# A batched transposing matmul: stores issued two batches sooner, and the first load of a in one transfer

## The chip, the core and the metric

One core of one Trainium2 chip. The metric is the device time in microseconds of one execution of the kernel, as the median of three runs. Five engines work side by side, each with its own instruction stream: PE (matmul), DVE (vector), ACT (scalar), POOL and SP. SP and ACT also issue DMAs, each into its own hardware queue, and 16 DMA engines serve both queues.

## The reference

Sixteen independent products of 512 x 512 matrices in float32; both operands come transposed.

```python
batch, m, k, n = 16, 512, 512, 512
a: [batch, k, m] float32        b: [batch, n, k] float32
out = np.matmul(a.transpose(0, 2, 1), b.transpose(0, 2, 1))   # [batch, m, n] float32
```

a and b are 16.8 MB each, and so is the output.

## The kernel before

Batches are handled in eight pairs (H = 8, B = 16). Every batch goes through these stages:

- **Loads (SP, q1).** b is loaded a pair at a time (2 MB, rows of 16 KB to a partition) into one of three buffers. a is loaded a pair at a time for pairs 1 to 5 (`WIDE`, 2 MB, rows of 16 KB), and a batch at a time for batches 0, 1 and 12 to 15 (1 MB, rows of 8 KB), into one of three pair buffers. Batch 0's a goes in two transfers, partitions 0 to 15 and partitions 16 to 127, both counted on the same semaphore.
- **Casts to bf16.** ACT casts a (`cast_a`, L168 and L170), DVE casts b (`cast_b`, L193).
- **Transposing b (PE, L246).** b in bf16 is seen as float32 words, so that one transpose turns two numbers at once; DVE copies the result from PSUM to SBUF (`turn`, L202).
- **Matmuls (PE, L260).** A batch is done in two halves of eight matmuls each. Each matmul group of four raises `summed` by one, so that `summed` is 4 for every finished batch.
- **Copies out (L180).** DVE copies the first half from PSUM into the output buffer, ACT the second half. There are five output buffers of one pair each (`OUTS`).
- **Stores (L89).** A pair is stored in one transfer of 2 MB (rows of 8 KB). Pairs 0 to 4 are stored from ACT's queue (q10): in `run_act`, behind the copy out of batch i, the pair j is stored for which i = 2j + 1 + LAG. With LAG = 3 pair 0 is stored behind the copy of batch 4. Pairs 5, 6 and 7 are stored by SP, behind all its loads; pair 7 in two transfers of one batch each.

Everything is ordered by hand with semaphores, and each engine runs its own program in order. What the steps of the prediction touch:

- ACT's order for batch i is: cast of batch i + 1, copy out of batch i (which waits until PE has summed all four parts of batch i), then possibly a store.
- DVE's order for pair p is: cast of the first half of pair p + 1's b, copy out of batch 2p, turn; cast of the other half, copy out of batch 2p + 1, turn.
- SP's order is that of the batches. Ahead of the loads of a for batches 10, 12 and 14 it waits until the store of pair 0, 1 and 2 has landed (its output buffer is to be used again). Ahead of a load into a used buffer of a it waits for PE (`summed`), and ahead of a b for the transposes (`turned`).
- SP's stores at the end wait for `summed`: pair 5 for the third part of batch 12, pair 6 for the third part of batch 14, the first half of pair 7 for the first part of batch 15, its second half for the last copies.

Of the kernel before, what the change touches and what calls it, by code (L numbers as in the profile page):

```python
# [11 lines left out]
def kernel(  # L12
# [7 lines left out]
    P = 128  # L20
    B, K, M = a.shape
    _, N, _ = b.shape
    KO = K // P
# [12 lines left out]
    a_v = a.rearrange("b (ki ko) m -> b ki ko m", ko=KO)  # L36
# [4 lines left out]
    WIDE = range(1, 6)  # L41
    LOADS = 3
    PAIRS = 3
    OUTS = 5
    LAG = 3
    TAIL = 3
    H = B // 2
    STORED = H - (H - OUTS) + 1
# [5 lines left out]
    with tc.tile_critical(sync_engine=nc.gpsimd.engine):  # L54
# [3 lines left out]
        a_sb = [sb(f"a_sb{s}", [P, 2 * KO, M], f32) for s in range(LOADS)]  # L58
# [12 lines left out]
        a_in = [sem(f"a_in{s}") for s in range(2 * LOADS)]  # L71
# [22 lines left out]
        def load_a(sp, i):  # L94

            q, g = divmod(i, 2)
            s, use = q % LOADS, q // LOADS
            if use:

                sp.wait_ge(summed, MO * (2 * (q - LOADS) + 1) + 1)  # L100
            if i == 0:

                for part in (slice(0, 16), slice(16, P)):
                    sp.dma_start(a_sb[s][part, :KO], a_v[0, part]).then_inc(a_in[0], 16)
            elif q in WIDE:
                sp.dma_start(a_sb[s][:], a_w[q]).then_inc(a_in[2 * s], 16)
            else:
                sp.dma_start(a_sb[s][:, g * KO:(g + 1) * KO], a_v[i]).then_inc(a_in[2 * s + g], 16)

        def loaded_a(q, g):  # L110

            g = 0 if q in WIDE else g
            uses = [u for u in range(q + 1) if u % LOADS == q % LOADS and (g == 0 or u not in WIDE)]
            return a_in[2 * (q % LOADS) + g], 16 * (len(uses) + (q % LOADS + g == 0))

        def run_sp(sp):
            for i in range(B):
                if i == 0:
                    load_a(sp, 0)


                for p in ([0] if i == 0 else [(i + 1) // 2] if i % 2 and i + 1 < B else []):
                    if p >= PAIRS:
                        sp.wait_ge(turned, p - PAIRS + 1)
                    sp.dma_start(b_sb[p % PAIRS][:], b_v[p]).then_inc(b_in[p % PAIRS], 16)
                if i % 2 == 0 and i // 2 >= OUTS:

                    sp.wait_ge(o_out[i // 2 % OUTS], 16 * (i // 2 // OUTS))
                if i and not (i % 2 and i // 2 in WIDE):
                    load_a(sp, i)  # L130

            for j in range(H - TAIL, H - 1):
                sp.wait_ge(summed, MO * (2 * j + 2) + 3)
                store(sp, j)

            sp.wait_ge(summed, MO * (B - 1) + 1)
            sp.wait_ge(half_go, 1)
            store(sp, H - 1, slice(0, 1))
            sp.wait_ge(last_go, 3)
            store(sp, H - 1, slice(1, 2))  # L140
# [17 lines left out]
        def cast_a(act, i):  # L158


            q, g = divmod(i, 2)
            sem_, value = loaded_a(q, g)
            x, to = a_sb[q % LOADS], a_bf[i % 2]
            act.wait_ge(sem_, value)
            if q in WIDE:
                own = slice(g * P // 2, (g + 1) * P // 2)
                for s in range(2):
                    copy = act.copy(to[s * P // 2:(s + 1) * P // 2], x[own, s * KO:(s + 1) * KO, :])  # L168
            else:
                copy = act.copy(to[:], x[:, g * KO:(g + 1) * KO, :])  # L170
            copy.then_inc(ac_go, 1)

        def copy_out(eng, i, rm, go):

            q = rm if isinstance(rm, int) else rm.stop - 1
            eng.wait_ge(summed, MO * i + q + 1)
            copy = eng.copy if eng is nc.scalar else eng.tensor_copy
            h = q // 2
            p = rm - 2 * h if isinstance(rm, int) else slice(None)
            copy(o_sb[i // 2 % OUTS][:, i % 2, rm, :], o_ps[h][:, p, :]).then_inc(go, 1)  # L180
# [40 lines left out]
        def run_act(act):  # L221
            cast_a(act, 0)
            for i in range(B - 1):
                cast_a(act, i + 1)
                copy_out(act, i, slice(2, 4), oa_go)
                j, odd = divmod(i - LAG, 2)
                if odd and 0 <= j < H - TAIL:
# [94 lines left out]
```

## Time and profile before

| | |
|---|---|
| median of 3 runs | 125.56 us (125.41 to 125.62) |
| the profiled execution | 125.41 us, span 123.5 us |
| mean granted TensorE clock | 0.948 |
| PE busy | 83.8 us (68%) |
| ACT busy | 66.9 us (54%) |
| DVE busy | 56.0 us (45%) |
| bytes moved | 50.33 MB |
| first store's issue on ACT | 45.0 us |
| last copy out ends | 114.5 us |

The span runs from the first to the last profiled instruction; what lies around it is 1.9 us. In the page's strip of 40 slices a slice is 3.1 us, and a digit is a share in tenths. A row of the group table has busy time, mean duration and the idle time ahead of it with the one that ended it. A row of a queue has packets, MB and the time of its packets as a share of 16 engines' time. In a table by stretch the columns are PE, PE's weight loads, DVE, ACT and POOL busy time with the number of instructions, then the granted clock, the DMA engines' share and GB/s.

### The profile page before, as it was taken

What the parts mean: (1) busy time and instruction counts of PE and PEld (TensorE: products, weight loads), DVE (VectorE), ACT (ScalarE), POOL (GpSimd) and SP (SyncE); (2) the same over time, 40 slices, a digit from 0 to 9 for tenths busy, and PEclk for the clock granted to TensorE, in tenths of its full rate; (3) what the DMA queues carried; (4) which work ended last, traced back from release to release, by engine and by line L of the source; (5) the groups of instructions that cost most, each with busy time, mean ns of one, the idle gap of its engine ahead of it and who ended that gap; (6) DMA issues with size and microseconds to landing.
All of it is one profiled execution on the core that took longest, in us unless ns stands there. A gap on an engine that the chain in (4) does not pass through costs nothing. (4 is left out here: it accounts for less than half of the span.)

```text
span 123.5 us, 1086 instructions
## 1 busy us (share of the span) xinstructions
PE 83.8 (68%) x392; PEld 48.1 (39%) x400; DVE 56.0 (45%) x48; ACT 66.9 (54%) x44; POOL 0.7 (1%) x6
## 2 busy tenths in 40 slices
PE   0000749799979979997996950595999499798000
PEld 0000733275546437445644620133744364374000
DVE  0002552829575592965759340039296543703000
ACT  4060006293999799799889008995320773803000
POOL 2000000000000000000000000000000000000000
PEclk9999999999999999999999999559999999999955
DMA  5989999999999999999999999999999999999992
GB/s 88 337 382 440 430 424 430 435 430 424 424 424 424 424 424 432 411 430 432 454 390 456 422 440 419 427 422 462 393 424 435 424 427 432 427 427 427 427 424 90
DMA packets 4944, 50.33 MB, mean 407 GB/s; under 512 B 464, under 2 KB 464, under 8 KB 464
## 3 DMA queue, kind: packets, MB, share of 16 engines
q1 hardware_dynamic: 3584, 39.85, 77.3%
q10 hardware_dynamic: 1360, 10.49, 20.1%
HBM read 33.55 MB, written 16.78 MB: 407 GB/s over the span
## 5 line engine op out<-in xcount | busy, mean ns | idle before, releaser
L260 PE MATMUL o_ps<-bt_sb,a_bf 128*128 128x512 bf16 x248 | 64.1, 407 | 9.5 <-PEq L235 8.5
L260 PEld LDWEIGHTS o_ps<-bt_sb,a_bf 128*128 128x128 bf16 x256 | 29.0, 116 | 39.9 <-issue 18.3
L168 ACT CAST a_bf<-a_sb 64x2048 bf16<-64x2048 f32 x20 | 38.0, 1898 | 6.8 <-DMA a_sb<-in_a_dram 6.5
L246 PE MATMUL bt_ps<-identity,b_bf 128*128 128x128 f32 x144 | 22.1, 302 | 20.5 <-PEq L235 20.5
L180 DVE COPY o_sb<-o_ps 128x1024 f32<-128x1024 f32 x16 | 19.6, 1224 | 30.7 <-PE o_ps L260 30.7
L246 PEld LDWEIGHTS bt_ps<-identity,b_bf 128*128 128x128 f32 x144 | 20.5, 209 | 25.4 <-issue 24.2
L193 DVE CAST b_bf<-b_sb 128x2048 bf16<-128x2048 f32 x16 | 19.4, 1219 | 22.9 <-DMA b_sb<-in_b_dram 22.9
L180 ACT COPY o_sb<-o_ps 128x1024 f32<-128x1024 f32 (+1 forms) x17 | 16.4, 965 | 19.7 <-PE o_ps L260 19.6
L170 ACT CAST a_bf<-a_sb 128x2048 bf16<-128x2048 f32 x6 | 11.4, 1900 | 20.2 <-DMA a_sb<-in_a_dram 20.2
L202 DVE COPY bt_sb<-bt_ps 128x1024 f32<-128x1024 f32 x16 | 19.4, 1215 | 2.7 <-PE bt_ps L246 2.7
L170 ACT ACT_TABLE_LOAD x1 | 1.3, 1283 | 0.9 <-PEq L306 0.9
L147 POOL TENSOR_SCALAR_AFFINE_SELECT identity<-identity 128x128 f32<-128x128 f32 x1 | 0.3, 296 | 0.2 <-POOL identity L145 0.2
L145 POOL MEMSET identity<- 128x128 f32 x1 | 0.2, 205 | 0.7 <-POOLq L54 0.7
L306 POOL MEMSET const-uint8-127<- 128x1 uint8 x1 | 0.1, 103 | 0.0
L306 POOL MEMSET const-bfloat16-1.0<- 128x1 bf16 x1 | 0.1, 102 | 0.0
L306 POOL MEMSET const-float32-0.0<- 128x1 f32 x1 | 0.1, 99 | 0.2 <-issue 0.2
L306 POOL MEMSET const-float32-1.0<- 128x1 f32 x1 | 0.1, 99 | 0.0
## 6 DMA issues: line engine op xcount, KB each, us to landing
b_sb<-in_b_dram SPq DMA_DIRECT2D x8, 2048.0 KB, 20.2
a_sb<-in_a_dram SPq DMA_DIRECT2D x5, 2048.0 KB, 18.3
out_dram<-o_sb ACTq DMA_DIRECT2D x5, 2048.0 KB, 16.2
a_sb<-in_a_dram SPq DMA_DIRECT2D x5, 1024.0 KB, 16.7
out_dram<-o_sb SPq DMA_DIRECT2D x2, 2048.0 KB, 13.3
out_dram<-o_sb SPq DMA_DIRECT2D x2, 1024.0 KB, 8.9
a_sb<-in_a_dram SPq DMA_DIRECT2D x1, 896.0 KB, 5.6
a_sb<-in_a_dram SPq DMA_DIRECT2D x1, 128.0 KB, 3.1
```

The lines of the kernel that those rows point to most:

```text
L145: pool.memset(identity[:], 0.0).then_inc(id_go, 1)
L147: pool.affine_select(out=identity[:], in_=identity[:], compare_op=mybir.AluOpType.not_equal, fill=1.0, base=0, pattern=[[-1, P]], channel_ ...
L168: copy = act.copy(to[s * P // 2:(s + 1) * P // 2], x[own, s * KO:(s + 1) * KO, :])
L170: copy = act.copy(to[:], x[:, g * KO:(g + 1) * KO, :])
L180: copy(o_sb[i // 2 % OUTS][:, i % 2, rm, :], o_ps[h][:, p, :]).then_inc(go, 1)
L193: dve.tensor_copy(to, x).then_inc(bc_go, n)
L202: dve.tensor_copy(bt_sb[g][:].rearrange("p j (ni r) -> p j ni r", r=NR), bt_ps[:].rearrange("p j r (g ni) -> p g j ni r", g=2)[:, g],).the ...
L246: last = pe.transpose(bt_ps[:, j, r, :], w[:, r, j, :], identity[:])
L260: last = pe.matmul(o_ps[h][:, q, :], a_r[:, rk, 2 * h + q, :], bt_h[:, rk // 2, rk % 2, :], start=(rk == 0), stop=(rk == KO - 1),)
L306: nc = _bacc.Bacc("TRN2", target_bir_lowering=False, num_devices=1)
```

## The change

Two edits. LAG goes from 3 to 1, so that the store of pair j is issued by ACT behind the copy out of batch 2j + 2 instead of batch 2j + 4. And batch 0's a is loaded by one transfer of 128 partitions, as the other single batches are, with its semaphore count adapted.

```diff
-    LAG = 3
+    LAG = 1
...
-            if i == 0:
-
-                for part in (slice(0, 16), slice(16, P)):
-                    sp.dma_start(a_sb[s][part, :KO], a_v[0, part]).then_inc(a_in[0], 16)
-            elif q in WIDE:
+            if q in WIDE:
                 sp.dma_start(a_sb[s][:], a_w[q]).then_inc(a_in[2 * s], 16)
             else:
                 sp.dma_start(a_sb[s][:, g * KO:(g + 1) * KO], a_v[i]).then_inc(a_in[2 * s + g], 16)
...
-            return a_in[2 * (q % LOADS) + g], 16 * (len(uses) + (q % LOADS + g == 0))
+            return a_in[2 * (q % LOADS) + g], 16 * len(uses)
```

The loop that LAG steers, the same before and after:

```python
            for i in range(B - 1):
                cast_a(act, i + 1)
                copy_out(act, i, slice(2, 4), oa_go)
                j, odd = divmod(i - LAG, 2)
                if odd and 0 <= j < H - TAIL:
                    store(act, j)
```

## The prediction

> **What bounds the kernel now.** I read the page first: the forty slices and the DMA queues.
>
> ```profile
> span 123.5 us, 1086 instructions
> ...
> DMA  5989999999999999999999999999999999999992
> ...
> q1 hardware_dynamic: 3584, 39.85, 77.3%
> q10 hardware_dynamic: 1360, 10.49, 20.1%
> HBM read 33.55 MB, written 16.78 MB: 407 GB/s over the span
> ```
>
> The DMA engines are busy in all slices but the first and the last. q1 is SP's queue (33.55 MB of loads and the last three pairs' stores), q10 is ACT's (five stores of 2.10 MB). From 12 us to 121 us the table by stretch gives 422 to 431 GB/s whatever the mixture, so I use 424. The bytes don't change; the end can only move if engines idle at the start, or run dry at the end. So next the tail, in the out_dram answer and the timeline.
>
> ```profile
> L89 SPq DMA_DIRECT2D out_dram<-o_sb x4: 344/366/403, 94.7 to 114.5; - x4
> DMA to landing us min/median/max: 8.0/14.4/18.3
> ```
>
> ```profile
> 96.37 1.90 ACT L170 CAST a_bf<-a_sb 128x2048 bf16<-128x2048 f32 x1 [3.60 <-DMA a_sb<-in_a_dram]
> ...
> 98.57 2.00 PE L260 MATMUL o_ps<-bt_sb,a_bf 128*128 128x512 bf16 x8 [0.90 <-PEq L235]
> ...
> 113.90 0.59 ACT L180 COPY o_sb<-o_ps 128x512 f32<-128x512 f32 x1 [0.32 <-PE o_ps L260]
> ```
>
> The last store (batch 15, 1.05 MB) is issued at 114.5 and lands 8.0 us later, at 122.5. The engines stop moving bytes at 121.1 (the stretch 121 to 122 has a share of 0.07), and 1.05 MB takes 2.5 us, so its bytes began at about 118.7: it stood 4.2 us behind other stores. That is the tail's whole cover. The first two lines of the timeline are the start of the last uninterrupted run of compute: batch 13's a lands at 96.4, ACT casts it at once, PE starts its first half 2.2 us after the landing, and from there to the last issue is 114.5 - 98.57 = 15.9 us with no wait for a load. So the last issue is batch 13's landing plus 18.1 us.
>
> How the queues share is read in the stretches around the first store, issued on ACT at 45.0: 44.8 to 48.5, 48.5 to 55.5, and 63.2 to 66.7 after a load was issued at 63.31.
>
> ```profile
> q1 hardware_dynamic: 115, 1.62, 103.1%
> ```
>
> ```profile
> q1 hardware_dynamic: 132, 1.90, 63.5%
> q10 hardware_dynamic: 128, 1.05, 35.3%
> ```
>
> ```profile
> q10 hardware_dynamic: 180, 1.47, 99.5%
> ```
>
> For 3.5 us after its issue the store moves nothing. Then loads of 16 KB rows get 1.90 MB in 7 us and the store 1.05 MB: about 2 to 1. The two loads that landed beside stores did so 7.4 us apart (55.7, 63.2) against 4.9 us alone (33.8, 38.7, 43.5). Beside loads of 8 KB rows (batches 12 to 15) it is near 1 to 1. In the third stretch q1 is empty: today SP waits for store 0 to land before it issues pair 5's a.
>
> ```profile
> SPq L108 <- DMA out_dram<-o_sb: 17.7, 2, 12.0
> SPq L106 <- DMA out_dram<-o_sb: 15.3, 1, 15.3
> ```
>
> **The change, part by part.** *The stores.* Store j of the five is issued when PE ends batch 2j+2 instead of 2j+4. No instruction and no semaphore wait is added; an issue takes 0.38 us on ACT's queue and moves ahead of two casts and two copies, while the ACT engine still works off its cast, so I cost that at nothing (uncovered it would be 0.4 us). What moves is bandwidth. PE ends batch 2 at 34.4 (32.68 + 1.75 in the timeline): store 0 is issued there, and moves bytes from 34.4 + 3.5 = 38, against 48.6 now. From then on loads go at the shared pace. Pair 3's b still lands at 38.7; behind it, 7.4 us each: pair 3's a 46.3 (now 43.5), b of pair 4 53.7 (48.4), its a 61.1 (55.7), b of pair 5 68.5 (63.2), its a 75.9, b of pair 6 83.3. Pair 5's a comes 1.4 us later only (now 74.5), since store 0 lands at 38 + 14.7 = 52.7 (14.7 us, as from 48.6 to 63.3 now) and SP issues that load then, not at 63.3: q1 doesn't run empty.
>
> Does q10 stay full? Stores start at 38, 52.7, 67.4, 82.1. Store 1 is issued at 45.0, store 2 at 55.5 (PE's end of batches 4 and 6; pair 3's a at 46.3 is before its cast at 47.04). Batch 8 needs the a that lands at 61.1: casts of 3.8 us, then two halves of 1.9, so store 3 is issued at 68.7. Batch 10 needs the a of 75.9: 75.9 + 3.8 + 3.8 gives store 4 at 83.5. All are there in time, so stores run without a break to the end of the loads. SP's gates for the remaining loads (store 1 landed, 67.4, for batch 12; store 2 landed, 82.1, for batches 14 and 15) also come before their turn in the queue.
>
> Then batch 12 at 1 to 1, 4.9 us: 88.2 (now 85.25). b of pair 7, 7.4: 95.6 (91.1). Batch 13, 4.9: 100.5 (96.35). Today store 3 begins to move only at 88.2 and store 4 at 99.9, so batch 13 passes with three and a half stores done; now it passes with almost all five. Batch 13 is 4.15 us later, bounds 3 (stores a little slower) and 6 (all five through). Pair 7's b doesn't bind: cast 1.2, copy 1.2, turn 1.2, transposes 1.2 end near 100.6, the cast of batch 13 at 102.4. Batch 14's a (105.0, cast 106.9) is before its need at 107.6, batch 15's (107.5) too. So the last issue goes to 114.5 + 4.15 = 118.7.
>
> Meanwhile the stores that covered it are gone: behind the last load only stores 5, 6 and 7 are left, 6.3 MB or 14.8 us. The last store's bytes begin at 118.7 + L, where L is the latency from issue to bytes, against 118.7 now. The loss is 4.15 + L - 4.2, about L. The trace has L at 3.5 us with the engines full (the store above), where most of it may be queueing, and about 1.0 with them idle:
>
> ```profile
> GB/s 0 0 0 0 0 0 0 0 0 0 0 0 0 0 0 590 459 0 0 328 393 131 0 131 131 66 66 0 328 524 197 524 459 393 328 328 131 459 393 66
> ```
>
> This is the first 5 us in slices of 0.125: the first load, issued at 0.89, moves at 1.9. Engines about to run dry are nearer to the idle row; as store 7's first half is still in flight I take 1.6. The tail costs 4.15 + 1.6 - 4.2 = 1.55 us, with ends at 0 (batch 13 only 3 us later, L 1.0: covered) and 5.3 (6 and 3.5). Store 6 goes at 106.3 + 4.15 = 110.5 plus L, as store 5's bytes end at about 111.2: a gap of 0.9, swallowed by the later one.
>
> The Trainium skill's page "DMA: Bandwidth & Descriptors", section "Latency and other measured facts", puts the first byte of such a transfer at about 600 ns; the trace's idle row is longer, 1.0, and its full row longer still. By that figure the tail would cost about 0.55 us, an estimate from that page.
>
> *The first load.* Two transfers (16 partitions, then 112) become one; SP saves one issue of 0.45 us, and everything behind goes out that much sooner. In the slices above, 131 KB move at 1.9 to 2.1, nothing for a quarter of a microsecond, and the bulk starts at 2.45. In one transfer the bulk can start at about 2.0, with 131 KB more in it (0.31 us at 424 GB/s): net -0.14. Bounds: -0.45 (the early piece bought nothing) and +0.31 (the larger transfer starts no sooner). I take -0.1. It is seen in full, for the whole span follows it.
>
> Sum against the profiled execution: 125.41 + 1.55 - 0.1 = 126.9 (the span 123.5 becomes 125.0, 1.9 lies around it). The median of the runs is 0.15 above that execution; I leave it inside the rounding.
>
> **Rivals.** *The PE clock falls in the last run of compute.* Once in this trace PE had nothing for 5.9 us:
>
> ```profile
> 72.70:76.60 3.90, 0.07 (x1) 0.00 (x0) 0.00 (x0) 2.06 (x2) 0.00 (x0) 1.00 1.01 431
> 76.60:83.40 6.80, 4.77 (x12) 1.70 (x13) 1.25 (x2) 6.55 (x4) 0.00 (x0) 0.50 1.00 426
> ```
>
> The granted clock fell 3.9 us into it and came back 4.8 us after matmuls resumed at 78.63. In the new timing batch 12's matmuls end between 97.1 and 99.2 and batch 13's start at 102.7, so 3.4 to 5.6 us without a matmul, against 3.0 now (95.6 to 98.57). If it falls, 4.8 us at half clock lose 2.4: 129.3. Against it: an earlier stall at pair 6 moves batch 12 towards 99.2. The Trainium skill, "TensorE: Matmul & The Clock Gate", section "Part 4: PE-mode transpose", says that transposes don't count as busy for this clock; the start of this trace agrees (16 transposes from 13.1, yet matmuls at half pace until 22.0). By that rule pair 7's transposes between the two don't keep the clock; if they did, this rival would fall away.
>
> *The tail stays covered.* If store 4 or 3 is late, or batch 13 is under 3 us later, no engine runs dry: 125.41 with the start's -0.1, so 125.3 to 125.6. For it: the full DMA digits of the profile. Against it: cover of 4.2 less L is all there is.
>
> *Faster.* One mechanism: the removed issue brings the bulk of the loads forward by the whole 0.45 us, at the start, and the tail is covered: 125.41 - 0.45 = 125.0. It decides if the late chain slips by less than 4.2 - L.
>
> **Chances.** Forecast 0.53, clock 0.2, covered 0.17, faster 0.1. A measurement can tell about 0.2% from no change, 0.25 us. The range goes from 125.3 (covered) to 129.3 (clock; L at 3.5 alone gives 128.8). Faster 0.1; same 0.13, most of the covered case; slower 0.77, with the rest of it.
>
> **What would show it.** Right: q10 moves from about 38 us; pair 3 to 5 loads 7.4 us apart and pair 5's a issued near 53; batch 13 landed near 100.5, the last issue near 118.7, and a dip in the DMA digits behind 111 us. Wrong: the last issue at 116 or sooner, or no dip (covered); a clock of 0.5 between 100 and 108 us (clock); the first bytes' bulk later than 2.45 us (the split was worth something).

## The result and the profile after

The changed kernel takes 128.34 us (128.15 to 128.5, 4 runs) against 125.52 us (4 runs): a ratio of 1.0225, 95% interval 1.0207 to 1.0242. The direction and the main mechanism of the forecast hold; the loss is 2.8 us where 1.3 were forecast. The profiled execution took 128.15 us, 2.7 more than the one of before.

The page of the changed kernel: span, clock and DMA in 40 slices of 3.16 us, and the stores' rows.

```profile
span 126.3 us, 1085 instructions
...
PEclk9999999999999999769999959999999855999996
DMA  3999999999999999999999999999999999909975
...
out_dram<-o_sb ACTq DMA_DIRECT2D x5, 2048.0 KB, 20.4
...
out_dram<-o_sb SPq DMA_DIRECT2D x2, 2048.0 KB, 10.6
out_dram<-o_sb SPq DMA_DIRECT2D x2, 1024.0 KB, 4.4
```

There is a hole now in the DMA row, the 0 at slice 36, from 110.5 to 113.7 us, and the last two slices (7 and 5) aren't full either. SP's small stores land 4.4 us after their issue (the median) instead of 8.9: they hardly stand behind others any more.

The table by stretch of the changed kernel shows the hole; the last three columns are clock, DMA share and GB/s.

```profile
106.00:110.00 4.00, 3.93 (x20) 2.23 (x19) 2.36 (x2) 0.60 (x1) 0.00 (x0) 0.89 1.01 428
110.00:114.00 4.00, 3.92 (x17) 1.74 (x16) 1.73 (x2) 2.81 (x2) 0.00 (x0) 1.00 0.18 74
114.00:118.00 4.00, 3.13 (x19) 2.27 (x19) 0.64 (x2) 1.01 (x1) 0.00 (x0) 1.00 1.03 426
118.00:122.00 4.00, 2.65 (x15) 1.52 (x14) 1.21 (x1) 1.17 (x2) 0.00 (x0) 1.00 0.87 360
```

From 110 to 114 us PE works all the time, while the DMA engines have 0.18 of their time filled: nothing is left to move until PE has summed enough of batch 14 for store 6. Before the change the share was full to 121 us:

```profile
100.00:108.00 8.00, 7.07 (x34) 3.73 (x33) 4.71 (x4) 5.57 (x4) 0.00 (x0) 1.00 1.02 431
108.00:121.00 13.00, 5.72 (x31) 3.79 (x32) 1.22 (x1) 1.43 (x3) 0.00 (x0) 0.87 1.01 428
```

The timeline of the changed kernel at batch 13, and the out_dram answer for SP's stores:

```profile
101.99 1.90 ACT L166 CAST a_bf<-a_sb 128x2048 bf16<-128x2048 f32 x1 [6.94 <-DMA a_sb<-in_a_dram]
...
104.19 3.23 PE L256 MATMUL o_ps<-bt_sb,a_bf 128*128 128x512 bf16 x8 [1.50 <-PEq L231]
```

```profile
L89 SPq DMA_DIRECT2D out_dram<-o_sb x4: 345/367/403, 97.0 to 121.4; - x4
```

Batch 13's a lands at 102.0 (96.4 before); the cast had waited 6.9 us for it. The first half of batch 13 starts 2.2 us after the landing, as before, but takes 3.23 us instead of 2.00. The last store is issued at 121.4, not 114.5: 6.9 us later, of which 5.6 are the landing and 1.2 the slower half.

### The profile page after: what moved, and what is told of

Read it like the earlier page. It is cut to its first block, busy times and chain, and to the rows that moved or that the text cites. A ratio compares the mean times of both kernels' runs of the same rounds, so it can differ in the third digit from the quotient of the medians.

```text
span 126.3 us, 1085 instructions
## 1 busy us (share of the span) xinstructions
PE 84.5 (67%) x392; PEld 49.1 (39%) x400; DVE 56.1 (44%) x48; ACT 66.7 (53%) x44; POOL 0.7 (1%) x6
## 3 DMA queue, kind: packets, MB, share of 16 engines
q10 hardware_dynamic: 1360, 10.49, 19.6%
## 5 line engine op out<-in xcount | busy, mean ns | idle before, releaser
L242 PE MATMUL bt_ps<-identity,b_bf 128*128 128x128 f32 x144 | 23.3, 313 | 26.9 <-PEq L231 26.9
L189 DVE CAST b_bf<-b_sb 128x2048 bf16<-128x2048 f32 x16 | 19.5, 1221 | 32.5 <-DMA b_sb<-in_b_dram 32.5
L242 PEld LDWEIGHTS bt_ps<-identity,b_bf 128*128 128x128 f32 x144 | 21.4, 210 | 31.9 <-issue 30.8
L198 DVE COPY bt_sb<-bt_ps 128x1024 f32<-128x1024 f32 x16 | 19.4, 1215 | 2.3 <-PE bt_ps L242 2.3
```

Of the source, the lines that this page charges most:

```text
L189: dve.tensor_copy(to, x).then_inc(bc_go, n)
L198: dve.tensor_copy(bt_sb[g][:].rearrange("p j (ni r) -> p j ni r", r=NR), bt_ps[:].rearrange("p j r (g ni) -> p g j ni r", g=2)[:, g],).the ...
L242: last = pe.transpose(bt_ps[:, j, r, :], w[:, r, j, :], identity[:])
```

## The experiments

Times are medians; each ratio is to the kernel before on the same chip (125.4 to 125.5).

**Each part alone.** First only the first load:

```diff
-    LAG = 1
+    LAG = 3
```

> Only the first load in one transfer, LAG stays 3. Theory (the start's gain is real, 1.1 us by the landings of b for pair 0, 10.60 against 11.70, and the engines' work at the end still covers the last store): 125.5 - 1.1 = 124.4, 124.2 to 124.8. Rival (as predicted, the start is worth 0.1 us and the earlier landings are given back): 125.2 to 125.6.

Measured: 124.39 us, ratio 0.9914 (0.989 to 0.9938). The theory holds: the first load in one transfer is worth 1.1 us where the end is covered. Batch 13's a lands at 96.6, and the last store, issued at 116.8, still stands behind others.

Then only the stores, on the kernel before:

```diff
-    LAG = 3
+    LAG = 1
```

> Only LAG 1, the first load stays in two transfers. Theory (the end hangs on batch 13's a, which lands when its own bytes and those of all the stores ahead of it are through; a start 1.1 us later delays the stores too, so fewer of their bytes come ahead of it): 128.0 to 129.0, the start's gain hardly seen. Rival (the two parts simply add): 128.3 + 1.1 = 129.4, 129.2 to 129.8.

Measured: 128.57 us, ratio 1.0249 (1.0182 to 1.0317), with executions from 127.8 to 129.6. The median fits the theory and is below what adding would give, but 129.4 would be a ratio of 1.031, inside the interval: that the parts don't simply add is not shown. Batch 13's a landed at 102.5, 0.5 us later than in the changed kernel, and that landing differs by more from one execution to the next (101.2 to 102.7, below). The theory's reason doesn't hold: up to that landing q10, the stores' queue, had moved 10.48 MB, against 10.49 MB in the changed kernel, so the later start left no fewer bytes of stores ahead of it.

**What sets the end.** TAIL 4 takes store 4 from ACT's queue and puts it behind SP's loads; the other four stores stay early.

```diff
-    TAIL = 3
+    TAIL = 4
```

> The changed kernel with TAIL 4: store 4 goes behind the loads on SP's queue, stores 0 to 3 stay early on ACT's. Theory (what counts is the bytes of stores ahead of batch 13's a and the bytes left behind the last load): batch 13's a lands about 5 us sooner, near 97, the engines don't run dry, 124.4, 124.2 to 124.8. Rival (early stores slow the loads and stall the compute all the way, whatever is left for the end): 126.5 to 128.3.

Measured: 124.54 us, ratio 0.9927 (0.9903 to 0.995). The whole loss is gone, though store 0 goes at 33.6 us (sooner than with LAG 1 and the split load, 34.8) and the loads beside the stores are as slow as in the changed kernel. Batch 13's a landed at 96.7. The same stretches as above, of this kernel:

```profile
106.00:110.00 4.00, 3.66 (x16) 1.58 (x14) 2.12 (x2) 2.92 (x3) 0.00 (x0) 1.00 1.01 428
110.00:114.00 4.00, 3.47 (x22) 2.67 (x23) 0.65 (x2) 0.71 (x1) 0.00 (x0) 1.00 1.02 430
114.00:118.00 4.00, 2.25 (x12) 1.13 (x11) 0.82 (x1) 1.17 (x2) 0.00 (x0) 1.00 1.01 426
118.00:122.00 4.00, 0.00 (x0) 0.00 (x0) 0.00 (x0) 0.00 (x0) 0.00 (x0) 0.76 0.63 264
```

The share stays at 1.01 to 1.02 until 118. Early stores as such do no harm here; what does is that all five are through ahead of batch 13's a.

Then half the step:

```diff
-    LAG = 1
+    LAG = 2
```

> The changed kernel with LAG 2. Theory: stores start 5 us later than with LAG 1, 0.75 MB fewer ahead of batch 13's a, which lands some 1.8 us sooner (near 100.2); the gap of the engines ahead of store 6 shrinks by as much: 126.4, 125.6 to 127.2. Rival (a threshold: any earlier store does the whole damage, or none): 128.3 or 124.4.

Measured: 124.38 us, ratio 0.9911 (0.9888 to 0.9934). My number was missed, and the time is the one that I gave to "none of the damage". The trace says why: batch 13's a landed at 98.3, not 100.2 (store 0 goes at 38.1 us, 6.7 later than with LAG 1; store 4 lands at 104.9, well behind batch 13's a, and 1.29 MB fewer of stores come ahead of it, not 0.75), and the last store goes at 117.8. The DMA rows of this kernel from 110 to 124 us, in slices of 0.35 us:

```profile
DMA  9999889999898999998999927998999900000000
GB/s 468 515 398 398 374 374 421 492 515 398 374 421 374 374 468 562 398 398 374 398 398 421 445 94 304 421 398 374 374 374 374 375 0 0 0 0 0 0 0 0
```

The 2 at the 24th slice, 118.1 us, is the moment at which store 7's first half ends and the second has just been issued. LAG 2 uses up the cover to the last tenths and pays nothing. So it is no threshold in the stores but the end of a cover, which is larger than I had it. The profiles give its size (the third column is what q10 had moved when batch 13's a landed):

| kernel | store 0 issued | q10 by then, MB | batch 13's a landed | last store issued | span | span behind the last issue |
|---|---|---|---|---|---|---|
| before | 45.0 | 8.06 | 96.4 | 114.5 | 123.5 | 9.0 |
| first load whole, LAG 3 | 42.1 | 8.39 | 96.6 | 116.8 | 122.4 | 5.6 |
| LAG 1, TAIL 4 | 33.6 | 8.39 | 96.7 | 117.0 | 122.7 | 5.7 |
| LAG 2 | 38.1 | 9.20 | 98.3 | 117.8 | 122.7 | 4.9 |
| changed (LAG 1) | 31.4 | 10.49 | 102.0 | 121.4 | 126.3 | 4.9 |
| LAG 1, split load | 34.8 | 10.48 | 102.5 | 121.9 | 126.8 | 4.9 |

The landing follows the bytes of stores ahead of it, not the time of the first store. In these profiles the span is never shorter than the last issue plus 4.9 us (3.9 to the landing, 1.0 behind it), nor shorter than what I take for the engines' time for all bytes: 122.4 to 122.7 with the quick start, 123.5 with the slow one. The kernel before had 9.0 - 4.9 = 4.1 us of cover. In rows two to four the last store goes 19.5 to 20.2 us behind batch 13's landing, not 18.1, and the span doesn't show it: that is the cover at work.

**The clock.** The changed kernel's slow half at 104 us falls into a clock of 0.5. To take that away I let PE sum the last quarter of batch 12 six times (the same values) while it waits, with the last two passes of its loop written out; a control has the loop written out only. `pair` is the loop's body as a function, and hands its argument to the second half of batch 12.

```diff
-                for q in range(2):
+                for q in [0] + [1] * (1 + again):
...
-                    last.then_inc(summed, 1)
+                    if q == 0 or again == 0:
+                        last.then_inc(summed, 1)
+                    again -= q
...
-            with pe.Fori(0, H) as _i:
+            with pe.Fori(0, H - 2) as _i:
+                pair()
+            pair(5)
+            pair()
```

The control, with pair(0) in place of pair(5):

> The changed kernel with the last two passes of PE's loop written out, nothing else; the control of the next run. All theories: 128.3, 127.9 to 128.7.

Measured: 128.16 us, ratio 1.0186 (1.0149 to 1.0224), one execution at 127.29.

> As the control, and PE sums the last quarter of batch 12 six times over (five repeats of four matmuls, 4.3 us, the same values), so that it isn't without matmuls while it waits for pair 7's b and batch 13's a. Theory (the clock that fell at 100.1 us costs 1.2 us of the 2.8: the first half of batch 13 took 3.23 us against 1.99, and all of it is on the path to the last store): the clock stays at 1.0 past 104 us, the last store is issued near 120.1, 127.1, 126.8 to 127.5. Rival (the copies of DVE and ACT set the pace of the last run, not PE): 128.3.

Measured: 127.67 us, ratio 1.0184 (1.016 to 1.0208). In the trace it does what it was made for. The stretches from 100 to 106 us, of the control and then of the kernel with the repeats:

```profile
100.00:104.00 4.00, 1.58 (x10) 1.10 (x10) 0.64 (x1) 2.78 (x2) 0.00 (x0) 0.74 1.01 426
104.00:106.00 2.00, 2.00 (x7) 0.66 (x5) 0.00 (x0) 1.77 (x2) 0.00 (x0) 0.50 1.03 434
```

```profile
100.00:104.00 4.00, 4.00 (x22) 2.44 (x21) 1.25 (x2) 1.31 (x1) 0.00 (x0) 1.00 1.00 420
104.00:106.00 2.00, 1.45 (x8) 0.74 (x8) 0.00 (x0) 2.00 (x3) 0.00 (x0) 1.00 1.01 426
```

The clock stays at 1.00, and from the landing of batch 13's a (102.7) to the last issue (120.8) it is 18.1 us, as before the change; in the control it is 20.3 (101.2 to 121.5). But batch 13's a landed 1.5 us later in this execution. So both were measured again, in more executions:

> The control again, with more rounds, beside the kernel with the repeated sums: 128.2, 127.9 to 128.5 by all theories.

> The kernel with the repeated sums again, with more rounds. Theory (the clock costs 1.2 us on the path to the last store): 1.2 us below the control. Second theory (it costs that in the run of compute, but the landing of batch 13's a wanders by as much from one execution to the next, 101.2 to 102.7 us in the profiles so far, so that some 0.5 us are seen): 0.3 to 0.8 us below the control. Rival (no effect): within 0.2 us of it.

Measured: control 127.39 us, ratio 1.0155 (1.012 to 1.019), executions from 126.8 to 128.4; with the repeats 127.55 us, ratio 1.0168 (1.0134 to 1.0201), executions from 126.4 to 128.3. The control was to be near 128.2 and wasn't. Here too the trace has 18.1 us with the repeats (101.5 to 119.6) against 19.5 in the control (101.8 to 121.3). The times show no gain that can be told from none, as the rival has it; the traces show the run of compute shorter by 1.3 to 2.2 us. All ten executions of each, from both rounds, have means of 127.7 and 127.5: a gain of 0.2 us, give or take 0.6, so the 1.2 us that I gave the clock are not in the times. One thing bears on it: the two control executions that were profiled have the lowest mean granted clock of the control's ten (0.917 and 0.928; the others have 0.936 to 0.954), so the traces may show the control at its worst. The landing wanders (101.2 to 102.7 in five profiles of LAG 1 with the whole load), and not with the stores: q10 had moved 10.40 to 10.49 MB by then in all five. That this eats the gain is not shown. What the clock costs the changed kernel in the times stays open.

**Why the first load is worth 1.1 us.** Two other cuts of it, on the kernel before. By partitions in the middle:

```diff
-                for part in (slice(0, 16), slice(16, P)):
+                for part in (slice(0, 64), slice(64, P)):
```

> The kernel before with the first load cut at partition 64 instead of 16. Theory P (the 112-partition transfer is slow by its shape: its 8 KB packets took 423 ns against 309 ns of the 128-partition one, and 64 partitions spread evenly): 124.5, 124.2 to 124.8, b of pair 0 landed by 10.9. Theory I (a second issue ahead of everything, 0.45 us, and the ramp between the two transfers cost the 1.1): 125.5.

Measured: 126.49 us, ratio 1.009 (1.0065 to 1.0114). Neither theory's number: slower than the kernel before. By columns, with all partitions in each transfer:

```diff
-                for part in (slice(0, 16), slice(16, P)):
-                    sp.dma_start(a_sb[s][part, :KO], a_v[0, part]).then_inc(a_in[0], 16)
+                for part in (slice(0, KO // 2), slice(KO // 2, KO)):
+                    sp.dma_start(a_sb[s][:, part], a_v[0, :, part]).then_inc(a_in[0], 16)
```

> The kernel before with the first load in two transfers of all 128 partitions, half of the columns each (rows of 4 KB). Theory P: 124.5, 124.2 to 124.8, since both transfers have 128 partitions. Theory I: 125.5.

Measured: 124.69 us, ratio 0.9936 (0.9919 to 0.9952). So a second issue, with rows of 4 KB, costs 0.3 us; the rest is the shape. The stretch from 3.5 to 5 us, where hardly anything but this load is under way, of the kernel before (112 partitions), of the cut at 64, and of the whole load with LAG 3:

```profile
3.50:5.00 1.50, 0.00 (x0) 0.00 (x0) 0.00 (x0) 0.00 (x0) 0.00 (x0) 1.00 0.99 344
```

```profile
3.50:5.00 1.50, 0.00 (x0) 0.00 (x0) 0.00 (x0) 0.00 (x0) 0.00 (x0) 1.00 0.81 175
```

```profile
3.50:5.00 1.50, 0.00 (x0) 0.00 (x0) 0.00 (x0) 0.00 (x0) 0.00 (x0) 1.00 1.02 431
```

They move 344, 175 and 431 GB/s. In the second the engines are only 0.81 busy, as the first half ends there and the other begins; for a full share it would be 347, 216 and 423 GB/s. So a transfer over fewer partitions is slower for every byte, and 64 are worse than 112. It is the size of the loss, too: from 2 to 8 us the whole load's kernel moved 2.34 MB, the cut by columns 2.20, the kernel before 1.89 and the cut at 64 1.57. At 424 GB/s the last three are 0.3, 1.1 and 1.8 us behind the first, and their times are 0.3, 1.1 and 2.1 us longer. Why fewer partitions are slower no run shows. The Trainium skill's page "DMA: Bandwidth & Descriptors", section "Rules for kernel authors", says of two transfers to disjoint partition halves not to bother, since they serialize. These runs agree with the advice, and the price is more than waiting in line: the two halves cost 126.49 - 124.39 = 2.1 us.

Last, whether the start can be quicker still, with b of pair 0 issued by ACT (LAG 3, first load whole):

```diff
-                for p in ([0] if i == 0 else [(i + 1) // 2] if i % 2 and i + 1 < B else []):
+                for p in ([] if i == 0 else [(i + 1) // 2] if i % 2 and i + 1 < B else []):
...
         def run_act(act):
+            act.dma_start(b_sb[0][:], b_v[0]).then_inc(b_in[0], 16)
             cast_a(act, 0)
```

> LAG 3, first load whole, and b of pair 0 issued on ACT's queue beside it. If the ramp of the first microsecond is the issue order of SP, b of pair 0 and everything behind it come some 0.3 us sooner: 124.1, 123.9 to 124.3. Rival (the ramp is the engines' own first packets, 0.5 to 1.3 us each): 124.4 as with the whole first load alone.

Measured: 124.42 us, ratio 0.9912 (0.9895 to 0.9929): the rival's number, nothing gained. Pair 0's b came later, at 12.1 us for 10.7, as it now shares the engines with batch 0's a. The last store was issued at 114.0, 2.8 us sooner than with the whole load alone, and the span is no shorter for it (122.7 for 122.4): the end is covered. The best that was found is the first load whole at LAG 3 or 2 (124.4 us, 1.1 us under the kernel before), with LAG 1 and TAIL 4 next to it (124.5).

## Why the prediction came out as it did

**Right:** that the bytes set a floor and only the two ends can move the time; that stores two batches sooner slow the loads (7.3 to 7.6 us apart from pair 3's b to pair 6's); that pair 5's a is issued early, at 50.9, with q1 never empty; that the cover behind the last load is then gone. Q10 was full to the end, as worked out. A gap ahead of store 6 was forecast at 0.9 us; the engines stood still for some 3 us. TAIL 4 shows the mechanism by undoing it.

**The step that failed:** "Batch 13 is 4.15 us later", and "the last issue goes to 114.5 + 4.15 = 118.7". It went to 121.4, 6.85 later. Two terms make the 2.7 us that were missed:

*The landing* is 5.6 us later, close to the bound of 6 ("all five through"). These rows are what q10 had moved from the span's start to batch 13's landing, before and in the changed kernel:

```profile
q10 hardware_dynamic: 1032, 8.06, 19.8%
```

```profile
q10 hardware_dynamic: 1360, 10.49, 24.3%
```

Before, 3.8 stores were through and not "three and a half"; now all five are, 2.43 MB more, which is 5.7 us at 424 GB/s. My 4.15 us are 1.76 MB. I had given every store 14.7 us, so that store 4 would start at 96.8. The run with LAG 1 and the split load checks that, since its store 0 goes at 34.8, about where I had it (34.4): its stores landed at 53.4, 67.4, 81.4, 93.0 and 103.7. The first three are as forecast; store 3 took 11.6 us, beside loads with rows of 8 KB, for which my own rows had near 1 to 1. Its row and that of store 2 (issued at 70.19 and 55.85; the last number is us to landing):

```profile
out_dram<-o_sb ACTq DMA_DIRECT2D x1, 2048.0 KB, 25.5
```

```profile
out_dram<-o_sb ACTq DMA_DIRECT2D x1, 2048.0 KB, 22.8
```

So store 4 started some 4 us sooner than in my sum and was as good as through. (A slip of 0.2: pair 3's a is 38.7 + 7.4 = 46.1, not 46.3.)

*The run of compute* is 1.2 us longer in this trace, 19.4 us for 18.1. That is the rival to which I gave 0.2, at half its price of 2.4, and its sign is there: 6.3 us without a matmul (97.9 to 104.2), transposes between them, and the clock at 0.51 from 100 to 104 us. I had set it aside because an earlier stall would push batch 12 to 99.2; it ended at 97.9. Whether the times, and not only the traces, carry its 1.2 us is the point left open above.

In the changed kernel store 0 went at 31.4, 3.0 us sooner than I had it: 1.1 are the quicker start of the stream, which I held for 0.1, and 1.6 the first batch's matmuls, as the transposes and matmuls of the start show, before and then changed:

```profile
13.10 3.66 PE L246 MATMUL bt_ps<-identity,b_bf 128*128 128x128 f32 x16 [13.10 <-PEq L235]
18.51 5.42 PE L260 MATMUL o_ps<-bt_sb,a_bf 128*128 128x512 bf16 x16 [1.75 <-PEq L235]
```

```profile
11.99 3.29 PE L242 MATMUL bt_ps<-identity,b_bf 128*128 128x128 f32 x16 [11.99 <-PEq L231]
17.04 3.81 PE L256 MATMUL o_ps<-bt_sb,a_bf 128*128 128x512 bf16 x16 [1.76 <-PEq L231]
```

PE's pace doubled at 22.0 us before and at 14.7 in the changed kernel; this is read from its instructions, since the profile's clock column has 1.00 in both stretches. That head start is not what makes batch 13 late: with the split load there is none, and the bytes of stores ahead are the same. But the start speaks against the rule on transposes that I took up in the clock rival and found confirmed in the kernel before. In the changed kernel the pace rose when PE had run nothing but transposes, and all sixteen matmuls behind them ran at the full pace.

**The cover** was mis-sized the other way: 4.2 - 1.6 = 2.6 us in my sum, 4.1 by the profiles, partly because the latency from issue to bytes with idle engines is shorter than I took. The last store is 8.0 us from issue to landing before, and 3.9 where nothing stands ahead of it. Store 6 shows the latency: it is issued at 113.2 us, and this is the DMA row of the changed kernel from 108 to 116 us in slices of 0.2.

```profile
DMA  9898898899894630000000000000009399399696
```

The engines stand still until 114.0 to 114.2: some 0.9 us behind the issue, so the idle row (1.0) was the right one and my 1.6 too much by 0.7. The other 0.8 I put down to the 118.7 at which I had the last store's bytes begin: it rests on 121.1 as their end, and a few still moved until about 121.7 (a share of 0.04 from 121.5 to 122). The sum with the measured terms: 5.6 + 1.2 - 4.1 = 2.7, the difference of the two profiled executions. The cover's error took 1.5 us off the two others: the forecast would have been farther off without it, and that is luck.

**The start** was mis-sized by ten times, -0.1 for -1.1, and outside my bounds of -0.45 and +0.31: I priced the bytes and the issue and took the rate of 112 partitions for that of 128, though the kernel's own second stretch stood at 252 GB/s between 2.5 and 5 us. And "seen in full, for the whole span follows it" holds where the end is covered. In the changed kernel 0.2 us of it are left by the medians (128.34 for 128.57 with the split load), and the spread of the latter doesn't settle how much.

## What to carry to other kernels

In a kernel bound by its transfers, work held back for the end is the cover of the last computation: before issuing stores sooner, add up which loads they pass and how many bytes remain behind the last load. A change that pays alone may be worth less beside another; measure the parts apart. And a first transfer cut by partitions to start sooner can cost more than it starts.

## What the runs showed of the hardware

- From 3.5 to 5 us of the span a load over 64 or 112 partitions moved 175 and 344 GB/s where one over 128 moved 431, with the engines 0.81, 0.99 and 1.02 busy.
- Issue to first bytes took 0.9 us with idle engines (the store at 113.2) and more than 3.5 us with full ones (stores at 31.4 and 45.0), and no engine time was lost in the longer wait.
- A store beside loads with rows of 16 KB took 14.0 us, and one beside loads with rows of 8 KB, for a part of it, 11.6 (LAG 1, split load).
- PE's pace doubled for the first time between 14.7 and 23.3 us in the profiles, and in the changed kernel while it ran transposes alone (from 11.99 on; its first matmul starts at 17.04).
